# Kernel rows of two S5 blocks in one run of matmuls, an output matrix built an iteration sooner, and one buffer fewer for the gate tiles

## The chip, the cores and the metric

One core of a Trainium2 chip runs the whole kernel. A core has TensorE (PE: matmuls, with a queue of weight loads, PEld), VectorE (DVE), ScalarE (ACT), GpSimd (POOL) and SyncE (SP), each with its own queue of instructions that it takes in order; SP and POOL issue most of the DMAs here. The metric is device time in microseconds, median of several executions. A profile is one execution that the hardware profiler recorded.

## The reference

A decoder block: one input projection, a gated linear attention (GLA, four heads) and a grouped diagonal state-space layer (S5, 64 groups of 16 channels) side by side, merged by sigmoid gates, then an MLP. The change lies in S5, and in the last GLA tiles beside it:

```python
proj = xn @ w_in[l]
r = proj[..., V_END:R_END]
u = proj[..., A_END:U_END]
...
o = rmsnorm(o, gla_norm_g[l]).reshape(bsz, N_META + seq, GLA_VAL) * jax.nn.silu(r)
y_gla = o @ w_o_gla[l]
y_s = s5_ssm(pad(u), a_re[l], a_im[l], log_step[l], b_re[l], b_im[l],
             c_re[l], c_im[l], d_skip[l])[:, N_PAD:]
...
mixed = jax.nn.sigmoid(z_gla) * y_gla + jax.nn.sigmoid(z_ssm) * y_ssm
```

`s5_ssm` computes, for each group, x_t = Λ x_{t-1} + B u_t and y_t = Re(C x_t) + D u_t over 528 positions (16 meta tokens and 512 others).

## The kernel before

**Dense work.** The projections are done in slots. A slot is one tile of 128 output channels by 512 positions: 24 matmuls, since every product of two float32 numbers is made as three products of their rounded parts (high by high, high by low, low by high) over eight tiles of the contraction. A slot's weights are loaded by SP into `wraw`; ACT makes `whi`, DVE makes `wlo = wraw - whi` (line 179). Around the change the slots are of three kinds. `r0` to `r7` are GLA's gate tiles (`r_slot`, line 1307): the matmuls write a bank of `mm`; `o` (tile tag `ro`) is a tile of GLA's normalised output, read back from DRAM by SP; ACT takes the sigmoid; DVE multiplies `rs<-rs,mm` and `rs<-rs,ro`, ACT rounds the product to `ogh`, DVE makes the rest `ogl`. Then comes `z7`, a tile of merge gates, and the slots `o0` to `o7`, which multiply `ogh` and `ogl` with `w_o_gla` and use merge gates held in tiles `zt`.

**S5 blocks.** The 64 groups go in eight blocks of eight; they are counted from 0 here, so the seventh is block 6 and the eighth block 7. Positions are taken in 66 chunks of eight. `tables()` (line 1177) builds for a block, on DVE with one copy on ACT, the output matrix M2 (lines 1183 to 1191: a copy of column 0, a multiplication of 128x1024, and for each half of the groups one multiplication into `mta` and one subtraction) and the input matrix M1 (lines 1193 to 1197: two multiplications and two adds or subtractions from B and the powers `lam`). `turns()` makes the rotation table E in three steps. `kernels()` (line 1213) multiplies M2 with B's columns, BA: eight matmuls of 32 columns into one bank, copied by ACT to `krow` and `other`, joined by DVE (`COPY_PREDICATED`) and stored by POOL into `kpad` in DRAM, from which POOL loads the Toeplitz matrix M3. `scan()` multiplies M1 with the block's input U (16 small matmuls, `sm<-U,M`), rotates with E, runs the scan on DVE and gives the states X. `output()` multiplies U with M3 and X with M2; `turn_output()` transposes the result, which POOL stores.

**The loop.** Iteration b finishes block b and prepares `after`, block b+1. It runs `after.tables()` step by step between slots, then `after.turns()`, and behind the iteration's last dense slot, on PE in this order: `after.kernels()`, the U,M matmuls of `after.scan()`, and `blk.output()`. From iteration 4 (HEADS) on there are no heads of GLA left; the pool `po_` is opened there and holds `ogh`, `ogl`, `ro`, `rs` and `zt`. Blocks' tiles come from the pool `b5`, where M1, B and `krow` have one buffer and M2 has two. `wraw`, `whi` and `wlo` have three buffers each, `ro` four, and there are four banks of tag `mm` and four of `sm`.

**What sets the order.** PE's instructions keep the order of the program. On the other engines a scheduler orders the work of these iterations, from dependences and free buffers; DMAs on SP and POOL stand in the order that it gives them too. Every engine then runs its own list in order, and waits where an operand or a buffer isn't ready.

Of the kernel before, what the change touches and what calls it, by code (L numbers as in the profile page):

```python
# [17 lines left out]
P = 128  # L18
D = 1024
KT = D // P  # L20
SEQ = 512
# [4 lines left out]
HEADS = 4  # L26
# [13 lines left out]
NST = NCK - 1  # L40
GRP = 64
NST_N = 64
HG = 16
GB = 8
NBLK = GRP // GB
# [5 lines left out]
def hybrid_block(ctx: ExitStack, tc: tile.TileContext, io, out: bass.AP):  # L51
    nc = tc.nc
    V, S, G = nc.vector, nc.scalar, nc.gpsimd
# [18 lines left out]
    class InOrder:  # L72


        def __init__(self, engine):
            self.engine = engine
# [4 lines left out]
    def mk(pool, shape, dt=F32, tag=None, **kw):  # L81
        count[0] += 1
        name = f"{tag or 'x'}_{count[0]}"
        size = 1
        for n in shape[1:]:
            size *= n
        if pool not in lined or size % LINE == 0:
            return pool.tile(shape, dt, tag=tag or name, name=name, **kw)
        t = pool.tile([shape[0], -(-size // LINE) * LINE], dt, tag=tag or name, name=name, **kw)[:, :size]
        if len(shape) == 2:  # L90
            return t
        dims = " ".join("abcd"[: len(shape) - 1])
        return t.rearrange(f"p ({dims}) -> p {dims}", **dict(zip("abcd", shape[1:])))
# [425 lines left out]
    rows = mk(pxt, [P, NT], tag="xrows")  # L519
    scale_rows.append(mk(pxt, [P, T8, NCK], tag="xrowp"))  # L520
    V, S = InOrder(nc.vector), InOrder(nc.scalar)
# [219 lines left out]
    def fetch(n):  # L741
        if n < len(dense) and n not in ready:
            ready[n] = load_w(dense[n][0])[0]
# [17 lines left out]
    def slot():  # L761
        n = at[0]
        at[0] += 1
        for i in range(n, n + AHEAD + 1):
            fetch(i)
        dense[n][1](ready.pop(n))
# [63 lines left out]
    other = mk(q5, [P, GRP, HG], tag="other")  # L830
# [114 lines left out]
    b5 = pool("b5", stack=sb5, side="right")  # L945
# [7 lines left out]
    class Head:  # L953
# [199 lines left out]
        def turn_outputs(self):  # L1153
            for v in range(2):
# [5 lines left out]
                S.activation(oT, ps, AF.Copy, scale=vecs[:, V_GN + m : V_GN + m + 1])  # L1160
                nc.gpsimd.dma_start(og_dram[m], oT)

    class Block:


        def __init__(self, blk):
            self.blk = blk
            self.gs = slice(blk * GB, (blk + 1) * GB)

        def loads(self, queue=nc.sync):  # L1170

# [5 lines left out]
        def tables(self):  # L1177

            M1 = self.M1 = mk(b5, [P, GB, 2, NST_N], tag="M1", bufs=1)
            self.M2 = mk(b5, [P, GB, 9, HG], tag="M2", bufs=2)  # L1180
            B, (lr, li) = self.B, (self.lam[:, i].unsqueeze(2).to_broadcast([P, GB, 2, NST_N]) for i in range(2))
            sh = [P, GB, T8, HG]
            S.copy(self.M2[:, :, 0], CA[:, self.gs])
            lrb, lib = (L[:, 1:, self.gs].rearrange("p l g -> p g l").unsqueeze(3).to_broadcast(sh) for L in (Lr, Li))
            ca, cb = (C[:, self.gs].unsqueeze(2).to_broadcast(sh) for C in (CA, CB))
            V.tensor_mul(self.M2[:, :, 1:], ca, lrb)
            for g0 in (0, 4):
                gg = slice(g0, g0 + 4)
                ta = mk(b5, [P, 4, T8, HG], tag="mta")
                V.tensor_mul(ta, cb[:, gg], lib[:, gg])  # L1190
                V.tensor_sub(self.M2[:, gg, 1:], self.M2[:, gg, 1:], ta)
                yield
            V.tensor_mul(M1, B, lr)
            yield
            V.tensor_mul(B, B, li)
            V.tensor_sub(M1[:, :, 0], M1[:, :, 0], B[:, :, 1])
            self.made = V.tensor_add(M1[:, :, 1], M1[:, :, 1], B[:, :, 0])
            yield

        def turns(self):  # L1200

# [11 lines left out]
        def kernels(self, tag="sm"):  # L1213

            ps = bank(tag)
            for j in range(GB // 2):
                for e in range(2):
                    g = 2 * j + e
                    PE.matmul(ps[32 * j : 32 * j + 32, e * P : (e + 1) * P], BA[:, self.blk * GB + 2 * j : self.blk * GB + 2 * j + 2, :].rearrange("p g h -> p (g h)"), self.M2[:, g, 0:8, :].rearrange("p l h -> p (l h)"), start=True, stop=True)
            krow = mk(b5, [P, P], tag="krow", bufs=1)  # L1220
            other = mk(b5, [P, GB, NST], tag="v", bufs=1).rearrange("p g c -> p (g c)")[:, :P]
            S.copy(krow, ps[:, :P])
            S.copy(other, ps[:, P : 2 * P])
            V.copy_predicated(krow, odd, other)
            V.scalar_tensor_tensor(krow[:, :HG], i16, vecs[:, V_D + self.blk : V_D + self.blk + 1], krow[:, :HG], op0=ALU.mult, op1=ALU.add)
            nc.gpsimd.dma_start(kpad[self.gs].rearrange("g h l -> (g h) l")[:, 112:], krow)
# [80 lines left out]
    def r_slot(m):  # L1307
        def go(w):
            ps = bank("mm")
            feat_tile(w, xh, xl, NM, NT, ps)  # L1310
            o = mk(po_, [P, SEQ], tag="ro", bufs=4)
            nc.sync.dma_start(o, og_dram[m])
            sg_ = mk(po_, [P, SEQ], tag="rs", bufs=2)
            S.activation(sg_, ps, AF.Sigmoid)
            V.tensor_mul(sg_, sg_, ps)
            V.tensor_mul(sg_, sg_, o)
            split_hi(ogh[:, m], sg_)
            V.tensor_sub(ogl[:, m], sg_, f32(ogh)[:, m])

        dense.append((cols("w_in", C_R + m * P), go))  # L1320
# [16 lines left out]
    heads, blocks = [], [Block(b) for b in range(NBLK)]  # L1337
# [63 lines left out]
    V, S = nc.vector, nc.scalar  # L1401
    for b, blk in enumerate(blocks):
        if not b:
            continue
        this = heads[b] if b < HEADS else None
        last = heads[b - 1] if 0 < b <= HEADS else None
        after = blocks[b + 1] if b + 1 < NBLK else None
        if b == 1:
            with tc.issue_after(heads[0].held.ins):
                list(blk.turns())  # L1410
        following = after.tables() if after else iter(())
        slot()
        early = b < HEADS + 1 or not after
        if b > 1:
            if early:
                blocks[b - 1].turn_output()
            if b == 2:
                heads[0].turn_outputs()
            next(steps)
        if this:  # L1420
            this.decay_load()
            with tc.issue_after(this.taken.ins), tc.issue_after(heads[0].held.ins), tc.issue_after(last.keyed.ins):
                list(this.decays())
        if b > 1:
            if after:
                after.loads()
            next(following, None)
        slot()
        if b == 1:
            blk.kernels("mm")  # L1430
            steps = blk.scan()
            next(steps)
            blocks[0].output("mm")
            blk.kernel_loads()
        list(steps)
        if not early:
            blocks[b - 1].turn_output()
        if b == 1:
            after.loads()
        if last:  # L1440
            last.outputs()
            if not this:
                last.normalised()
        if this:
            with tc.issue_after(this.taken.ins):
                this.query_decay()
        next(following, None)
        if b < NBLK - 1:
            slot()
        if this:  # L1450
            with tc.issue_after(this.kept.ins):
                last.normalised()
            this.turn_values()
        next(following, None)
        if after:
            list(after.turns())
        slot()
        if this:
            this.turn_keys()
        if b == 1:  # L1460
            blocks[0].turn_output(tag="mm")
        if last and b > 1:
            last.turn_outputs()
        if b == HEADS:
            sgb.close()
            sg.close()
            so = ExitStack()
            po_ = pool("po", stack=so, padded=True)
            ogh = mk(po_, [P, KT, SEQ], F32R, tag="ogh")
            ogl = mk(po_, [P, KT, SEQ], F32R, tag="ogl")  # L1470
        for _ in range(2):
            next(following, None)
        if after:
            slot()
        if this:
            this.scores("mm")
        if after:
            after.kernels()
            steps = after.scan()
            next(steps)  # L1480
        blk.output("mm" if this else "sm")
        if after:
            after.kernel_loads()
        if this:
            this.states()
            this.split()
    slot()
    blocks[-1].turn_output(last=True)
    while at[0] < len(dense):
# [107 lines left out]
    for c4, c in enumerate(range(0, D, 256)):  # L1597
        ss_ = []
        parts = out_weights(c4, dict(raw_))
        for i, w in enumerate(load_w(wg[:, D + c : D + c + 256])):  # L1600
# [5 lines left out]
            zt = mk(pgl, [P, SEQ], tag="zi", bufs=2)  # L1606
# [161 lines left out]
    V, S = InOrder(nc.vector), InOrder(nc.scalar)  # L1768
# [110 lines left out]
    V, S = nc.vector, nc.scalar  # L1879
# [62 lines left out]
    po_ = pool("pout", side="right", padded=True)  # L1942
# [178 lines left out]
```

## Time and profile before

| | |
|---|---|
| median of 3 runs | 856.58 us (856.49 to 856.67) |
| the profiled execution | 856.36 us |
| its span, first to last instruction | 854.6 us |
| mean granted clock of TensorE | 0.998 |
| ACT busy | 466.1 us (55%) |
| POOL busy | 150.9 us (18%) |
| DMA, mean over the span | 225 GB/s |

The median is of unprofiled runs, the span of the one that was recorded; 856.36 − 854.6 = 1.76 us of it lie around the span. Blocks 6 and 7 are prepared between about 290 and 352 us of the span. In the rows, names of tiles are without their numbers, and both M1 and M2 (and M3) are called M: `M<-CA,Lr` and `M<-M,mta` are M2, `M<-B,lam` and `M<-M,B` are M1, `sm<-M,BA` are kernel rows (M2), `sm<-U,M` the scan's input (M1), `sm<-M,U` and `sm<-M,X` the output (M3, M2). A row of the timeline has start and duration in us, engine, line, operation, what is written from what is read, and in brackets how long the engine was idle before and who ended that.

### The profile page before, as it was taken

The page shows a single profiled execution, that of the slowest core. Times are in us where ns is not written, and L with a number is a line of the kernel's source. Part 1 is how long each engine was busy: PE and PEld are TensorE (multiplying, and loading weights), DVE is VectorE, ACT ScalarE, POOL GpSimd, SP SyncE. Part 2 cuts the span into 40 slices and gives each one's busy share as a digit, 9 for nine tenths or more (in the row PEclk, how much of TensorE's full clock was granted, in tenths as well). Part 3 has the DMA queues.
Part 4 walks back from the last instruction along what each step waited for, and adds up shares of the span by engine and source line. Part 5 has one row for each costly group of instructions (what it writes and reads, how often), then busy time and mean ns, then how long its engine had stood idle before and what let it go on. Part 6 is the DMA issues. An engine that isn't in the chain of part 4 may idle for free.

```text
span 854.6 us, 13817 instructions
## 1 busy us (share of the span) xinstructions
PE 845.5 (99%) x4974; PEld 725.7 (85%) x4974; DVE 688.9 (81%) x1282; ACT 466.1 (55%) x832; POOL 150.9 (18%) x265
## 2 busy tenths in 40 slices
PE   9999999999999999999999999999999999999996
PEld 8998889898988888888888889888888888888885
DVE  6999889998989599846888687667666777688886
ACT  7677465766856546334555466333222246885763
POOL 1123120240303123240222421011111100000001
PEclk9999999999999999999999999999999999999999
DMA  9887765566565765686898996498989967766564
GB/s 316 194 279 225 226 148 150 141 162 178 138 165 153 242 187 144 223 267 204 242 281 265 280 281 217 134 331 289 346 280 333 363 218 243 267 192 197 172 200 145
DMA packets 172492, 192.67 MB, mean 225 GB/s; under 512 B 18648, under 2 KB 127720, under 8 KB 172424
## 3 DMA queue, kind: packets, MB, share of 16 engines
q1 hardware_dynamic: 145040, 109.66, 44.3%
q0 software_dynamic: 25408, 77.93, 27.4%
q10 hardware_dynamic: 1976, 4.20, 1.6%
q8 instruction: 39, 0.64, 0.3%
q14 instruction: 29, 0.24, 0.1%
HBM read 149.52 MB, written 42.24 MB: 224 GB/s over the span
## 4 chain that ended last, share of the span: by engine, by line
PE 96%; DMA 2%; DVE 1%; ACT 0%; issue 0%; SPq 0%; DVEq 0%; ACTq 0%
PE mm L61 72%; PE sm L61 22%; PE sm L66 2%; DMA wraw<-in_w_in_dram 2%; DMA xT<-in_x_cols_dram 1%; DVE c L2041 0%; DVE c L2016 0%; DVE wlo L79 0%; ACT whi L79 0%; DVE rl L79 0%; DVE xT L79 0%; ACT rh L79 0%; DVEq L2117 0%; SPq L478 0%; DVE ff_r L150 0%
## 5 line engine op out<-in xcount | busy, mean ns | idle before, releaser
L164 ACT ACTIVATE whi<-wraw 128x1024 fp32r<-128x1024 f32 x81 | 85.8, 1059 | 180.4 <-PE mm L61 171.2
L61 PE MATMUL mm<-xh,whi 128*128 128x512 f32 (+2 forms) x464 | 157.5, 339 | 0.0
L61 PE MATMUL mm<-xh,wlo 128*128 128x512 f32 (+2 forms) x464 | 155.2, 335 | 0.0
L61 PE MATMUL mm<-xl,whi 128*128 128x512 f32 (+2 forms) x464 | 155.1, 334 | 0.0
L179 DVE TENSOR_TENSOR wlo<-wraw,whi 128x1024 fp32r<-128x1024 f32 x81 | 98.9, 1223 | 69.1 <-ACT whi L164 69.0
L61 PE MATMUL mm<-hh,whi 128*128 128x512 f32 (+2 forms) x272 | 100.7, 370 | 0.0
L61 PE MATMUL mm<-hh,wlo 128*128 128x512 f32 (+2 forms) x272 | 100.6, 370 | 0.0
L61 PE MATMUL mm<-hl,whi 128*128 128x512 f32 (+2 forms) x272 | 100.6, 370 | 0.0
L61 PEld LDWEIGHTS mm<-xh,wlo 128*128 128x128 f32 x464 | 87.4, 188 | 9.0
L61 PEld LDWEIGHTS mm<-xh,whi 128*128 128x128 f32 x464 | 87.3, 188 | 8.8 <-issue 0.3
L61 PEld LDWEIGHTS mm<-xl,whi 128*128 128x128 f32 x464 | 87.3, 188 | 8.5
L1959 DVE TENSOR_TENSOR wlo<-wraw,whi 128x1024 fp32r<-128x1024 f32 x56 | 68.4, 1223 | 22.4 <-ACT whi L1955 22.2
L61 PE MATMUL sm<-wlo,fh 128*128 128x512 f32 x192 | 74.8, 390 | 0.0
L61 PE MATMUL sm<-whi,fl 128*128 128x512 f32 x192 | 74.7, 389 | 0.0
L61 PE MATMUL sm<-whi,fh 128*128 128x512 f32 x192 | 74.7, 389 | 0.0
L1955 ACT ACTIVATE whi<-wraw 128x1024 fp32r<-128x1024 f32 x56 | 58.7, 1050 | 17.1 <-PE mm L61 11.7
L61 PEld LDWEIGHTS mm<-hh,whi 128*128 128x128 f32 x272 | 51.1, 188 | 8.8
L61 PEld LDWEIGHTS mm<-hl,whi 128*128 128x128 f32 x272 | 51.1, 188 | 8.7
L61 PEld LDWEIGHTS mm<-hh,wlo 128*128 128x128 f32 x272 | 51.1, 188 | 8.7
L164 ACT ACTIVATE fh<-f 128x512 fp32r<-128x512 f32 x48 | 30.2, 629 | 36.1 <-PE sm L61 22.3
L61 PE MATMUL mm<-gh,whi 128*128 128x512 f32 x128 | 49.8, 389 | 0.0
L61 PE MATMUL mm<-gl,whi 128*128 128x512 f32 x128 | 49.8, 389 | 0.0
(537 smaller groups left out, 1880.8 us busy)
## 6 DMA issues: line engine op xcount, KB each, us to landing
wraw<-in_w_ff_dram SPq DMA_DIRECT2D x56, 512.0 KB
wraw<-in_w_in_dram SPq DMA_DIRECT2D x46, 512.0 KB
w2raw<-in_w_ff_dram POOLq DMA_DIRECT2D x16, 1024.0 KB, 8.8
t2d<-w2t POOLq DMA_DIRECT2D x16, 1024.0 KB, 6.0
wraw<-t2d SPq DMA_DIRECT2D x32, 512.0 KB
wraw<-in_w_glu_dram SPq DMA_DIRECT2D x16, 512.0 KB
M<-kpad POOLq DMA_DIRECT2D x64, 64.0 KB, 2.6
wraw<-in_w_o_gla_dram SPq DMA_DIRECT2D x8, 512.0 KB
```

The lines of the kernel that those rows point to most:

```text
L61: ins = nc.tensor.matmul(*args, **kw)
L66: ins = nc.tensor.transpose(*args, **kw)
L164: return S.activation(dst, src, AF.Copy, scale=scale)
L179: V.tensor_sub(lo, raw, f32(hi))
L1955: halved = S.activation(bh, raw, AF.Copy)
L1959: V.tensor_sub(bl, raw, f32(bh))
```

## The change

Four edits belong together.

- The part of `tables()` that builds M2 becomes a generator of its own, `outward(pl)`, which can take its tile from another pool. For block 7 it is run in whole at the end of iteration 4, from `po_`, with one buffer; `tables()` of block 7 then builds M1 alone, in iteration 6 as before.
- In iteration 5 block 7's kernel rows are made right behind block 6's, into a bank of tag `mm`. In iteration 6 `kernels()` is not called.
- The rows of block 7 go into a `zt` tile of `po_` (columns 0 to 127 for the rows, 128 to 255 for the other half) instead of `krow` and `v`.
- `ro` has three buffers instead of four.

```diff
+    JOINED = NBLK - 1
...
         def tables(self):
 
             M1 = self.M1 = mk(b5, [P, GB, 2, NST_N], tag="M1", bufs=1)
-            self.M2 = mk(b5, [P, GB, 9, HG], tag="M2", bufs=2)
             B, (lr, li) = self.B, (self.lam[:, i].unsqueeze(2).to_broadcast([P, GB, 2, NST_N]) for i in range(2))
+            if not self.M2:
+                yield from self.outward(b5)
+            V.tensor_mul(M1, B, lr)
+            yield
+            V.tensor_mul(B, B, li)
+            V.tensor_sub(M1[:, :, 0], M1[:, :, 0], B[:, :, 1])
+            self.made = V.tensor_add(M1[:, :, 1], M1[:, :, 1], B[:, :, 0])
+            yield
+
+        def outward(self, pl):
+
             sh = [P, GB, T8, HG]
+            self.M2 = mk(pl, [P, GB, 9, HG], tag="M2", bufs=2 if pl is b5 else 1)
             S.copy(self.M2[:, :, 0], CA[:, self.gs])
...
                 V.tensor_sub(self.M2[:, gg, 1:], self.M2[:, gg, 1:], ta)
                 yield
-            V.tensor_mul(M1, B, lr)
-            yield
-            V.tensor_mul(B, B, li)
-            V.tensor_sub(M1[:, :, 0], M1[:, :, 0], B[:, :, 1])
-            self.made = V.tensor_add(M1[:, :, 1], M1[:, :, 1], B[:, :, 0])
-            yield
...
-            krow = mk(b5, [P, P], tag="krow", bufs=1)
-            other = mk(b5, [P, GB, NST], tag="v", bufs=1).rearrange("p g c -> p (g c)")[:, :P]
+            if self.blk == JOINED:
+                rows = mk(po_, [P, SEQ], tag="zt", bufs=6)
+                krow, other = rows[:, :P], rows[:, P : 2 * P]
+            else:
+                krow = mk(b5, [P, P], tag="krow", bufs=1)
+                other = mk(b5, [P, GB, NST], tag="v", bufs=1).rearrange("p g c -> p (g c)")[:, :P]
...
-            o = mk(po_, [P, SEQ], tag="ro", bufs=4)
+            o = mk(po_, [P, SEQ], tag="ro", bufs=3)
...
         if after:
-            after.kernels()
+            if after.blk != JOINED:
+                after.kernels()
+            if b == JOINED - 2:
+                blocks[JOINED].kernels("mm")
             steps = after.scan()
...
+        if b == HEADS:
+            list(blocks[JOINED].outward(po_))
```

What this does to the order of instructions is seen in the built programs. Names carry numbers here; `mm_739` is a bank, M1, M2 and M3 are told apart.

On PE, behind the last dense slot of iteration 5, stands before (the second line is block 6's kernel rows, eight matmuls):

```order
L61 MATMUL mm_730_4223<-xh_7_100,wlo_709_4109 128x512
L61 MATMUL sm_733_4256<-M2_695_4040,BA_14_110 32x128 x8
L61 MATMUL sm_738_4274<-U_714_4148,M1_694_4039 64x65 x8
L61 MATMUL sm_739_4286<-U_714_4148,M1_694_4039 64x65 x8
L61 MATMUL sm_740_4298<-M3_685_3983,U_651_3792 64x128 x2
```

and at the same place in the changed program, where `M2_686` is block 7's output matrix:

```order
L61 MATMUL mm_733_4232<-xh_7_100,wlo_712_4118 128x512
L61 MATMUL sm_736_4265<-M2_698_4049,BA_14_110 32x128 x8
L61 MATMUL mm_739_4281<-M2_686_3992,BA_14_110 32x128 x8
L61 MATMUL sm_743_4298<-U_717_4157,M1_697_4048 64x65 x8
L61 MATMUL sm_744_4310<-U_717_4157,M1_697_4048 64x65 x8
L61 MATMUL sm_745_4322<-M3_685_3983,U_651_3792 64x128 x2
```

The third line has moved here from behind the last dense slot of iteration 6, where dense work is now followed by the scan's matmuls at once. The number of matmuls is the same.

On DVE, around the last operations of block 6's M1 (its two adds, `M1<-M1,B`), before:

```order
L1196 TENSOR_TENSOR M1_694_4039<-M1_694_4039,B_692_4034 128x8x64
L1318 TENSOR_TENSOR ogl_668_3875<-rs_712_4138,ogh_667_3874 128x512
L241 TENSOR_TENSOR E_713_4146<-mta_717_4163,epb_718_4164 128x8x16
L242 TENSOR_TENSOR E_713_4146<-mta_717_4163,epb_718_4164 128x8x16
L1197 TENSOR_TENSOR M1_694_4039<-M1_694_4039,B_692_4034 128x8x64
L239 TENSOR_TENSOR mta_719_4169<-E_713_4146 128x512
L240 TENSOR_TENSOR epb_720_4170<-E_713_4146 128x512
L1315 TENSOR_TENSOR rs_726_4208<-rs_726_4208,mm_724_4181 128x512
L241 TENSOR_TENSOR E_713_4146<-mta_719_4169,epb_720_4170 128x8x32
L242 TENSOR_TENSOR E_713_4146<-mta_719_4169,epb_720_4170 128x8x32
L1316 TENSOR_TENSOR rs_726_4208<-rs_726_4208,ro_725_4206 128x512
L179 TENSOR_TENSOR wlo_729_4221<-wraw_727_4217,whi_728_4219 128x1024
```

and in the changed program:

```order
L241 TENSOR_TENSOR E_716_4155<-mta_720_4172,epb_721_4173 128x8x16
L242 TENSOR_TENSOR E_716_4155<-mta_720_4172,epb_721_4173 128x8x16
L1328 TENSOR_TENSOR rs_729_4217<-rs_729_4217,ro_728_4215 128x512
L239 TENSOR_TENSOR mta_722_4178<-E_716_4155 128x512
L240 TENSOR_TENSOR epb_723_4179<-E_716_4155 128x512
L1330 TENSOR_TENSOR ogl_668_3875<-rs_729_4217,ogh_667_3874 128x512
L241 TENSOR_TENSOR E_716_4155<-mta_722_4178,epb_723_4179 128x8x32
L242 TENSOR_TENSOR E_716_4155<-mta_722_4178,epb_723_4179 128x8x32
L1189 TENSOR_TENSOR M1_697_4048<-M1_697_4048,B_695_4043 128x8x64
L1190 TENSOR_TENSOR M1_697_4048<-M1_697_4048,B_695_4043 128x8x64
L179 TENSOR_TENSOR wlo_732_4230<-wraw_730_4226,whi_731_4228 128x1024
L1327 TENSOR_TENSOR rs_735_4259<-rs_735_4259,mm_733_4232 128x512
```

The adds stood among the second rotation step, `rs` and `ogl`; now they stand behind the last rotation step, that `rs` and an `ogl` which came after the wlo. Between one and the same wlo further up (`wlo_688` before, `wlo_691` now, shown next) and the second add there are 54 rows where from that wlo through the `rs<-rs,ro` shown there were 50.

On DVE, some fifty rows earlier, at the start of that stage, before:

```order
L179 TENSOR_TENSOR wlo_660_3823<-wraw_658_3819,whi_659_3821 128x1024
L179 TENSOR_TENSOR wlo_671_3883<-wraw_669_3879,whi_670_3881 128x1024
L179 TENSOR_TENSOR wlo_688_3996<-wraw_686_3992,whi_687_3994 128x1024
L1315 TENSOR_TENSOR rs_674_3912<-rs_674_3912,mm_672_3885 128x512
L1224 COPY_PREDICATED krow_676_3927<-odd_18_114,v_677_3928 128x128
```

and in the changed program:

```order
L179 TENSOR_TENSOR wlo_660_3823<-wraw_658_3819,whi_659_3821 128x1024
L179 TENSOR_TENSOR wlo_671_3883<-wraw_669_3879,whi_670_3881 128x1024
L1200 TENSOR_TENSOR M2_686_3992<-CA_12_108,Lr_10_106 128x8x128
L1205 TENSOR_TENSOR M2_686_3992<-M2_686_3992,mta_687_3995 128x4x128
L179 TENSOR_TENSOR wlo_691_4005<-wraw_689_4001,whi_690_4003 128x1024
L1327 TENSOR_TENSOR rs_674_3912<-rs_674_3912,mm_672_3885 128x512
```

Two operations of block 7's M2 (`M2_686`) now stand ahead of that wlo.

More of the change, by code (lines that the diff above doesn't have):

```diff
@@ L1168, in __init__ @@
             self.gs = slice(blk * GB, (blk + 1) * GB)
+            self.M2 = None
         def loads(self, queue=nc.sync):
```

## The prediction

> **What bounds the kernel now.** I read the page first: the busy table and the chain of work that ended last.
>
> ```profile
> PE 845.5 (99%) x4974; PEld 725.7 (85%) x4974; DVE 688.9 (81%) x1282; ACT 466.1 (55%) x832; POOL 150.9 (18%) x265
> ...
> PE 96%; DMA 2%; DVE 1%; ACT 0%; issue 0%; SPq 0%; DVEq 0%; ACTq 0%
> ```
>
> TensorE (PE) is busy for 845.5 us of the 854.6 us span, and 96% of the chain that ended last is PE. Next I asked for the waits of PE, whole run, and then for busy time by window around the two places that the diff moves: 289.7 to 321.2 us is the stage that ends with block 6's kernel rows, 321.2 to 351.5 us the one that ends with block 7's.
>
> ```profile
> PE sm L61 <- DVE xss L517: 1.3, 1, 1.3
> PE sm L61 <- DVE xrs L79: 0.4, 1, 0.4
> ```
>
> ```profile
> core 0: us, PE busy (x) PEld busy (x) DVE busy (x) ACT busy (x) POOL busy (x), PEclk, DMA share, GB/s
> 289.70:321.20 31.50, 31.50 (x216) 26.00 (x214) 30.86 (x52) 15.77 (x29) 7.18 (x13) 1.00 0.68 207
> 321.20:351.50 30.30, 30.30 (x182) 25.04 (x178) 29.45 (x49) 14.27 (x27) 7.75 (x14) 1.00 0.62 180
> ```
>
> PE waits for other engines twice, both near the start (xss and xrs belong to the first norm). In the two stages it never stops. So the time changes in two ways only: PE's own instruction stream gets shorter or longer, or somebody is now late for PE. The candidate is VectorE (DVE): busy 30.86 of 31.50 us in the first stage, so nearly every operation put into it pushes out all that stands behind.
>
> **PE's own stream.** The change leaves all instructions and moves eight small matmuls. PE's timeline at three places, start and duration:
>
> ```profile
> 319.81 0.39 PE L61 MATMUL mm<-xh,wlo 128*128 128x512 f32 x1
> 320.13 0.67 PE L61 MATMUL sm<-M,BA 128*32 128x128 f32 x16
> 320.73 0.69 PE L61 MATMUL sm<-U,M 128*64 128x65 f32 x16
> ...
> 351.16 0.39 PE L61 MATMUL mm<-ogh,wlo 128*128 128x512 f32 x1
> 351.48 0.66 PE L61 MATMUL sm<-M,BA 128*32 128x128 f32 x16
> 352.07 0.34 PE L61 MATMUL sm<-U,M 128*64 128x65 f32 x4
> ...
> 371.67 0.39 PE L61 MATMUL mm<-ogh,wlo 128*128 128x512 f32 x1
> 371.99 0.44 PE L61 MATMUL sm<-M,U 128*64 128x128 f32 x4
> ```
>
> The record count is twice that of the program (each of the eight is two records). In the second place the run goes: from the last dense matmul to the scan's matmuls are 352.07 − 351.16 = 0.91 us before. Afterwards dense work is followed by a 64-column group at once; the third place shows that pair, 371.99 − 371.67 = 0.32. Saving **0.59 us**; bounds 0 (the whole gap stays) and 0.91.
>
> In the first place the run of 16 records becomes 32. The sixteen matmuls last 0.67 from first start to last end; a single one lasts 0.28 (mean of the form, below), so fifteen steps take 0.39, 0.026 each, and sixteen more steps cost **+0.42 us**. If the two banks' runs met as badly as M,BA meets U,M (first start to first start 0.60, of which 16 steps are 0.42, so 0.18 more), it would be +0.60; if they overlapped as much as possible, 0.39. By itself PE's stream comes out at 0.42 − 0.59 = **−0.17 us** (to +0.01 with the worse seam).
>
> ```profile
> L61 PE MATMUL sm<-M,BA 128*32 128x128 f32 x112 | 4.6, 279 | 0.0
> ```
>
> [...]
>
> **The new wait.** The scan's matmuls U,M read M1, block 6's input matrix, whose last two operations are the adds `M<-M,B`. DVE, in the first stage:
>
> ```profile
> 289.72 1.22 DVE L179 TENSOR_TENSOR wlo<-wraw,whi 128x1024 fp32r<-128x1024 f32 x1 [5.13 <-ACT whi L164]
> ...
> 296.24 0.69 DVE L1285 TENSOR_TENSOR qt<-q,sm 128x512 f32<-128x512 f32 x1 [0.48 <-ACT q L1283]
> ...
> 298.67 0.68 DVE L1190 TENSOR_TENSOR mta<-CB,Li 128x512 f32<-128x512 f32 x1
> 299.27 1.24 DVE L1258 TENSOR_TENSOR_SCAN v<-d,v 128x520 f32<-128x520 f32 x1
> ...
> 314.66 0.69 DVE L1196 TENSOR_TENSOR M<-M,B 128x512 f32<-128x512 f32 x1
> ...
> 316.27 0.69 DVE L1197 TENSOR_TENSOR M<-M,B 128x512 f32<-128x512 f32 x1
> ...
> 319.34 0.70 DVE L1316 TENSOR_TENSOR rs<-rs,ro 128x512 f32<-128x512 f32 x1
> 319.94 1.23 DVE L179 TENSOR_TENSOR wlo<-wraw,whi 128x1024 fp32r<-128x1024 f32 x1
> ```
>
> Before, the last add ends at 316.27 + 0.69 = 316.96, and PE takes U,M at 320.73: 3.8 us to spare. In the changed order both adds stand behind the last rotations, the next `rs<-rs,ro` and an `ogl`. From the wlo of 289.72 to the second add, both included, stand 54 rows: all 50 that stood from that wlo through 319.34, and four more (two `mta<-CB,Li`, one `M<-M,mta`, one `ogl<-rs,ogh`). Each such 128x512 operation takes 299.27 − 298.67 = 0.60 of DVE. Before, the 50 rows were through at 319.94. Four more make 2.40; the hole of 0.48 ahead of qt is filled, as two of the four now stand ready there. DVE is through at 319.94 + 2.40 − 0.48 = 321.86, and as an operation ends some 0.10 after the next may start (0.70 long, step 0.60), M1 is whole at **321.96** (322.44 if the hole stays).
>
> PE would want U,M at 320.73 + 0.42 = 321.15. It waits about 0.8 us, and with a few hundredths of signalling I take **+0.85** (bounds 0.4 and 1.35: one operation less in between, or the hole kept). Behind the waiting matmul stand U,M, the block output and the next dense run, that is all of PE, so the wait is paid in full and carried to the end, since PE waits nowhere later.
>
> Sum: +0.42 + 0.85 − 0.59 = **+0.68 us**. While there is a wait, the seam does not count: U,M starts when M1 is whole.
>
> **Edits that I cost at nothing.** The first two operations of block 7's output matrix on DVE stand in the idle 5.13 us ahead of 289.72. They take 1.13 and 0.60:
>
> ```profile
> 329.06 1.22 DVE L1186 TENSOR_TENSOR M<-CA,Lr 128x1024 f32<-128x1024 f32 x1
> 330.19 1.24 DVE L1258 TENSOR_TENSOR_SCAN v<-d,v 128x520 f32<-128x520 f32 x1
> ```
>
> If that cover were gone, M1 would be 1.73 later, and so would PE. The copies on ACT (column 0 of M2, two copies of rows) lie on an engine that is busy 15.77 of 31.50 us. POOL stores block 7's rows earlier, at 7.18 busy of 31.50. With three buffers for ro, a gate tile's load may be issued when the `rs<-rs,ro` three slots back is through; those stand some 5.6 us apart (313.72 and 319.34), so 16.8 us remain for an issue and a landing, and the longest median landing in the page's table of DMA issues is 11.4:
>
> ```profile
> 313.72 0.69 DVE L1316 TENSOR_TENSOR rs<-rs,ro 128x512 f32<-128x512 f32 x1
> ...
> woraw<-in_w_out_dram POOLq DMA_DIRECT2D x8, 512.0 KB, 5.0
> ...
> wraw<-tdo POOLq DMA_DIRECT2D x4, 512.0 KB, 11.4
> ```
>
> SP handles the loads in order, so a late ro would also hold the wraw behind it; it has the same 16.8 us.
>
> **The second place and block 7's B.** B has one buffer, so block 7's load waits for block 6's last add, and it moves with it:
>
> ```profile
> 316.99 0.60 SPq L895 DMA_DIRECT2D B<-bard  x1
> ...
> DMA to landing us min/median/max: 7.7/7.7/7.7
> ...
> 341.37 0.70 DVE L1318 TENSOR_TENSOR ogl<-rs,ogh 128x512 fp32r<-128x512 f32 x1
> ...
> 345.50 0.39 PE L61 MATMUL mm<-ogl,whi 128*128 128x512 f32 x1
> ```
>
> It was issued at 316.99, right behind the add; now at about 322.0. The one B load whose landing is shown took 7.7, so B is there at 329.7 (327.0 to 333.4 by the 5.0 and 11.4 of other 512 KB loads). In the new order `M<-B,lam` stands 14 rows behind the last add. Those are two wlo (319.94, the next operation of before starts at 321.08: 1.14), six of 0.60, the two halves of v (0.67 together) and the row operations of two blocks (0.20 + 0.15 each):
>
> ```profile
> 321.08 0.69 DVE L1318 TENSOR_TENSOR ogl<-rs,ogh 128x512 fp32r<-128x512 f32 x1
> ...
> 324.02 0.31 DVE L1224 COPY_PREDICATED krow<-odd,v 128x128 f32<-128x128 int32 x1
> 324.22 0.70 DVE L1316 TENSOR_TENSOR rs<-rs,ro 128x512 f32<-128x512 f32 x1
> 324.82 0.24 DVE L1225 SCALAR_TENSOR_TENSOR krow<-i,vecs,krow 128x16 f32<-128x16 f32 x1
> 324.97 0.77 DVE L1252 TENSOR_TENSOR v<-sm,E 128x260 f32<-128x260 f32 x2
> 325.64 0.69 DVE L1282 SCALAR_TENSOR_TENSOR q<-q,sm 128x512 f32<-128x512 f32 x1
> ```
>
> Together 7.25 us, so DVE gets there at about 329.1 and waits **0.6 us** (0 to 4.3). Does PE notice? Behind it on DVE is the last `ogl`, which PE reads first at 345.50, later by 0.42 + 0.85: 346.8. Counted from 319.94 as before, the work up to that ogl loses 4.1 us (five M2 operations, one ogl) and gains 2.7 (B's multiplication, two adds, two row operations); from 321.86 that ends at about 342.5 without the wait. So 4.2 us are free and I put down **0**.
>
> The profiled execution took 856.36, 0.22 under the median of 856.58. 856.36 + 0.68 = 857.04, on the median **857.3**.
>
> **The rivals.**
> - **No new wait**: DVE gains enough (rows that waited for ACT or PE before, or an earlier start) to finish M1 by 321.15. It needs 0.8 us, more than the hole of 0.48 already spent. Then −0.17: 856.4 (856.6 with the worse seam). Against it: the four operations are in the order and 30.86 of 31.50 is busy.
> - **Slower, by block 7's B**: the load lands late enough to hold DVE past its 4.2 us, that is after 329.1 + 4.2 = 333.3, 11.3 us past its issue. Then PE waits at the first ogl, us for us: at 13 us, 1.7 more, in all +2.4, 859.0. For it: landings of 11.4 exist at this size. Against: the only B load seen took 7.7, and the DMA share is 0.62 there.
> - **The second place saves nothing**: the scan's matmuls start no sooner behind dense work (the 0.91 was the change of shape, not the run). Then +0.42 + 0.85 = +1.27: 857.9. Against: 0.32 at 371.67.
>
> **How the numbers follow.** Forecast of a short wait (856.8 to 857.9): 0.76. No new wait: 0.12. Block 7's B: 0.06. No saving: 0.06. The range 856.2 to 858.4 takes in the first, the second and the fourth. 0.2% of the time, about what a measurement can tell from no change, is 1.7 us: faster is below 854.9, slower above 858.3. The forecast and the no-wait case lie within; slower is B's case and some 0.03 of a longer wait: 0.09. Faster needs a gain that no row shows: 0.03.
>
> **What would show it.** Right: a wait of PE on DVE's add of M1 (line 1190 of the new kernel) of 0.5 to 1.3 us near 321, thirty-two records of M,BA in a row, U,M about 0.3 behind dense work at the second place, B's load near 322 and a wait at `M<-B,lam` that nobody on PE answers. Wrong: no wait of PE there; a wait at the first ogl of the slots behind; a wlo that PE waits for; or a wait of 2.5 us, which would mean that the idle 5.13 us didn't cover M2's first operations.

## The result and the profile after

| | before | after |
|---|---|---|
| median of 7 runs | 856.58 us (856.26 to 856.67) | 859.30 us (857.22 to 860.86) |
| the profiled execution | 856.36 us | 860.06 us |
| its span | 854.6 us | 858.3 us |
| mean granted clock of TensorE | 0.998 | 0.995 |

The ratio of the runs is 1.0030, 95% interval 1.0020 to 1.0039: slower by about 2.6 us (the medians differ by 2.72). The runs of before lie within 0.41 us of each other; those of the changed kernel spread over 3.64. In the two later sessions the kernel before spread over 1.72 (29 runs) and 0.65 (13 runs).

The waits of PE for its whole run, after (engine and line waited for: us in total, times, longest):

```profile
PE sm L61 <- issue: 1.6, 1, 1.6
PE sm L61 <- DVE xss L517: 1.3, 1, 1.3
PE sm L61 <- DVE xrs L79: 0.3, 1, 0.3
PE sm L61 <- DVE M L1190: 0.3, 1, 0.3
PE sm L61 <- DVE wlo L79: 0.2, 1, 0.2
```

Three were not in the list of before. The last of them lies in the first 30 us, and the kernel with M1 early (first experiment), which loses nothing, has it too. The other two, "issue" and L1190, matter; PE's timeline shows both at one place, behind the joined kernel rows:

```profile
320.21 0.66 PE L61 MATMUL sm<-M,BA 128*32 128x128 f32 x16
320.67 0.66 PE L61 MATMUL mm<-M,BA 128*32 128x128 f32 x16
322.90 0.30 PE L61 MATMUL sm<-U,M 128*64 128x65 f32 x2 [1.57 <-issue]
323.45 1.09 PE L61 MATMUL sm<-U,M 128*64 128x65 f32 x29 [0.26 <-DVE M L1190]
...
327.85 0.55 PE L61 MATMUL mm<-xh,whi 128*128 128x512 f32 x1
```

The first half of M1 comes at 322.80 and lets two matmuls go (the view writes "issue", but they are the ones that read it, and in the kernel with the early matrix only it names the add, L1189); the second comes at 323.40 and lets the rest go. The next dense matmul starts at 327.85, 4.40 after that. The granted clock explains a part of these 4.40; busy time by window, the clock is the number behind the last bracket:

```profile
core 0: us, PE busy (x) PEld busy (x) DVE busy (x) ACT busy (x) POOL busy (x), PEclk, DMA share, GB/s
...
323.00:324.00 1.00, 0.74 (x20) 0.61 (x22) 1.00 (x2) 0.00 (x0) 0.00 (x0) 1.00 0.15 51
324.00:325.00 1.00, 1.00 (x29) 1.00 (x25) 1.00 (x2) 0.00 (x0) 0.00 (x0) 0.79 0.11 41
325.00:326.00 1.00, 1.00 (x12) 1.00 (x10) 1.00 (x4) 0.03 (x1) 0.00 (x0) 0.50 0.51 160
326.00:327.00 1.00, 1.00 (x14) 1.00 (x12) 0.99 (x4) 0.60 (x1) 0.57 (x1) 0.50 0.51 131
327.00:328.00 1.00, 1.00 (x10) 0.67 (x6) 0.81 (x3) 0.04 (x1) 0.23 (x1) 0.51 0.63 146
328.00:329.00 1.00, 1.00 (x5) 0.82 (x6) 0.41 (x1) 0.96 (x3) 0.31 (x1) 1.00 1.12 228
```

PE pays a second time: about a microsecond after the wait its clock is halved, for 3.4 us (the four windows lack 0.21 + 0.50 + 0.50 + 0.49 = 1.70 us of full clock). The page's line for the clock still shows nines there; only the fine windows tell.

DVE, which PE waits for, through the same stage:

```profile
284.58 1.22 DVE L1200 TENSOR_TENSOR M<-CA,Lr 128x1024 f32<-128x1024 f32 x1
285.83 0.69 DVE L1205 TENSOR_TENSOR M<-M,mta 128x512 f32<-128x512 f32 x1
289.80 1.23 DVE L179 TENSOR_TENSOR wlo<-wraw,whi 128x1024 fp32r<-128x1024 f32 x1 [3.27 <-ACT whi L164]
...
291.54 0.30 DVE L1236 COPY_PREDICATED krow<-odd,v 128x128 f32<-128x128 int32 x1
293.00 0.69 DVE L1328 TENSOR_TENSOR rs<-rs,ro 128x512 f32<-128x512 f32 x1 [1.17 <-DMA ro<-og]
...
295.63 0.69 DVE L1204 TENSOR_TENSOR mta<-CB,Li 128x512 f32<-128x512 f32 x1
296.66 0.69 DVE L1297 TENSOR_TENSOR qt<-q,sm 128x512 f32<-128x512 f32 x1 [0.35 <-ACT q L1295]
...
298.48 1.22 DVE L1200 TENSOR_TENSOR M<-CA,Lr 128x1024 f32<-128x1024 f32 x1
...
322.72 0.68 DVE L1190 TENSOR_TENSOR M<-M,B 128x512 f32<-128x512 f32 x1
```

and the rows of before at the same place:

```profile
291.46 0.29 DVE L1224 COPY_PREDICATED krow<-odd,v 128x128 f32<-128x128 int32 x1
291.89 0.69 DVE L1316 TENSOR_TENSOR rs<-rs,ro 128x512 f32<-128x512 f32 x1
...
294.54 1.22 DVE L1186 TENSOR_TENSOR M<-CA,Lr 128x1024 f32<-128x1024 f32 x1
```

Block 7's first two operations do lie in the idle stretch ahead of the wlo, which still has 3.27 us of its 5.13 left. But DVE then waits 1.17 for the first `ro` tile, where the profile of before shows no wait (it stood 0.14 there, from 291.75 to 291.89, and the view puts that down to nobody), and the hole ahead of `qt` stays.

The second place, dense work straight into the scan's matmuls:

```profile
355.50 0.39 PE L61 MATMUL mm<-ogh,wlo 128*128 128x512 f32 x1
355.82 0.57 PE L61 MATMUL sm<-U,M 128*64 128x65 f32 x12
```

0.32 instead of 0.91, as forecast. The difference between the two profiled executions, 3.70 us, is then made of: 0.08 from a slightly later start of the stage (320.21 against 320.13), 0.44 for the longer run of kernel rows (how it is measured: first experiment), 2.20 of wait (323.45, where PE without a wait would have been at 320.21 + 0.60 + 0.44 = 321.25; of these 2.20 PE stood idle for 1.57 + 0.26 = 1.83), 1.57 for the slow clock (4.40 where 2.83 is enough; below), and −0.59: together 3.70.

### The profile page after: what moved, and what is told of

It reads as the page before. It is cut to its first block, busy times and chain, and to the rows that moved or that the text cites. A ratio compares the mean times of both kernels' runs of the same rounds, so it can differ in the third digit from the quotient of the medians.

```text
span 858.3 us, 13818 instructions
## 1 busy us (share of the span) xinstructions
PE 847.3 (99%) x4974; PEld 727.3 (85%) x4974; DVE 689.8 (80%) x1282; ACT 465.8 (54%) x832; POOL 151.4 (18%) x265
## 4 chain that ended last, share of the span: by engine, by line
PE 94%; DMA 2%; DVE 2%; issue 0%; ACT 0%; ACTq 0%; DVEq 0%
PE mm L61 71%; PE sm L61 22%; PE sm L66 2%; DMA wraw<-in_w_in_dram 2%; DMA xT<-in_x_cols_dram 1%; DVE c L2058 0%; DVE ogl L1330 0%; DVE c L2033 0%; DVE rs L1328 0%; DVE wlo L79 0%; DVE epb L240 0%; DVE B L1188 0%; DVE wlo L179 0%; ACT whi L79 0%; ACT whi L164 0%
```

## The experiments

After the profile the theory was: the early output matrix pushes M1 of block 6 back on DVE, PE idles for it, and that idle time also halves PE's clock. The rivals: the joined rows, the third `ro` buffer or block 7's late B cost by themselves; and the slow stretch comes from the small matmuls or from memory traffic, not from idling.

### M1 finished ahead of the rotations

```diff
+        if b == JOINED - 2:
+            list(following)
         if after:
             list(after.turns())
```

> The changed kernel, with block 6's input matrix M1 finished ahead of block 6's rotations (its adds stand 16 rows earlier on DVE). Theory: all of the loss is PE's wait for M1 and what that wait sets off; without it PE's own stream remains, -0.2 to 0 us against before: 856.4 to 856.7, no wait of PE near 321, granted clock 1.00 throughout. Rival: the joined rows, the single late load of block 7's B or the third ro buffer cost by themselves; then 857.5 or more stays, with PE waiting elsewhere.

Measured: 856.15 us (11 runs, 855.84 to 856.65), before in the same session 856.39; ratio 0.9996 (0.9987 to 1.0004). PE has no wait between 280 and 400 us, and its clock is 1.00 from 280 to 333 us. Its timeline:

```profile
319.88 0.66 PE L61 MATMUL sm<-M,BA 128*32 128x128 f32 x16
320.34 0.66 PE L61 MATMUL mm<-M,BA 128*32 128x128 f32 x16
320.92 1.15 PE L61 MATMUL sm<-U,M 128*64 128x65 f32 x32
323.75 0.50 PE L61 MATMUL mm<-xh,whi 128*128 128x512 f32 x1
```

From the first kernel row to U,M are 1.04 us, 0.60 before: the longer run costs 0.44, and the seam between the banks is as long as the steps within them (by single records of the changed kernel's profile, where the two banks also start 0.46 apart, they come in fours, 0.11 apart, across the seam too: 320.45 and 320.56 in the first bank, 320.67 and 320.78 in the second). From U,M to dense work are 2.83, as before (320.73 to 323.56). With everything else of the change in, the time is that of before, or a little under, which this many runs can't tell. So the joined rows and the third `ro` buffer cost nothing that shows by themselves. Block 7's B is not late here: its load is issued right behind M1's last add (add over at 316.96 and load at 316.99 before, 323.40 and 323.43 in the changed kernel), and that add stands 16 rows earlier on DVE; that its lateness cost nothing in the changed kernel is seen in that kernel's own profile, where DVE takes B without a wait (below). DVE waited 1.6 us for the first `ro` here too, and it cost nothing, as PE had no wait for M1.

### PE kept busy during the wait

```diff
                 blocks[JOINED].kernels("mm")
+                fill = bank("mm")
+                for _ in range(8):
+                    PE.matmul(fill, xh[:, 0, :P], xh[:, 0, NM:NT], start=True, stop=True)
```

> The changed kernel with eight extra 128x512 matmuls (into a bank that nobody reads) behind the joined kernel rows, 1.8 us of PE work inside the wait of 2.2 us. Theory (idle PE halves the granted clock): the wait stays, M1 comes at the same time, but the clock stays at 1.00 and the 1.6 us of slow matmuls are not paid: 858.0 to 858.6, the runs close together. Rival (the slow stretch belongs to the small matmuls or to the memory traffic there): the stretch at 0.50 stays, 859 to 861 as in the changed kernel, spread over 3 us.

Measured: 858.49 us (11 runs, 857.84 to 859.77), under the changed kernel's 859.30 although PE does more. Its ratio to before is 1.0022 (1.0014 to 1.0031), and that interval overlaps the changed kernel's, so the times alone don't tell the two apart. The clock stays at 1.00 from 318 to 330 us in the profile, PE shows no wait there, and the profiled run took 858.12. Dense work starts 6.24 after the first kernel row (326.00 − 319.76); less the 2.83 from U,M to dense work, PE was let go 3.41 after that row, 3.24 in the changed kernel (323.45 − 320.21), so no earlier. The upper end of the spread is above what was expected (859.77 against 858.6); those runs were not profiled.

### Four buffers for ro again

```diff
-            o = mk(po_, [P, SEQ], tag="ro", bufs=3)
+            o = mk(po_, [P, SEQ], tag="ro", bufs=4)
...
-                zt = mk(po_, [P, SEQ], tag="zt", bufs=6)
+                zt = mk(po_, [P, SEQ], tag="zt", bufs=5)
```

The smaller `zt` (in three places, of which one is shown) makes room.

> The changed kernel with four buffers for ro again and five for zt instead of six. Theory: the wait of 1.2 us for the first ro is the chance of one landing, not of the buffer count; time as of the changed kernel, 858 to 861, a wait of PE of 1 to 2.3 us. Rival: the third buffer's loss delays ro; then the wait of DVE on ro goes, M1 comes 1.2 us earlier, PE waits about 1.0 and the time falls to 857.3 or lower.

Measured: 858.15 us (11 runs, 857.81 to 861.02); the wait of DVE for the first `ro` is still there, 0.9. The profiled run took 858.15, and is the changed kernel without the slow clock:

```profile
322.57 0.30 PE L61 MATMUL sm<-U,M 128*64 128x65 f32 x2 [1.29 <-issue]
323.12 1.09 PE L61 MATMUL sm<-U,M 128*64 128x65 f32 x29 [0.25 <-DVE M L1190]
...
325.95 0.50 PE L61 MATMUL mm<-xh,whi 128*128 128x512 f32 x1
```

The wait cost 1.92 us here (323.12, less 320.16 + 0.60 + 0.44), 0.28 less than in the changed kernel's profile (PE stood idle for 1.29 + 0.25 = 1.54 of it), the clock stayed at 1.00, and U,M to dense work took 2.83 instead of 4.40. Two of its eleven runs took 859.49 and 861.02. So the buffer count is not the cause of that wait. The kernel's ratio to before is 1.0022 (1.0013 to 1.0030), that of the changed kernel 1.0030 (1.0020 to 1.0039): the intervals overlap, and no difference is claimed.

### Only the three-buffer edit, in the kernel before

```diff
-            o = mk(po_, [P, SEQ], tag="ro", bufs=4)
+            o = mk(po_, [P, SEQ], tag="ro", bufs=3)
```

> The kernel before with three buffers for ro and nothing else; DVE's order is that of before. Theory: the buffer count costs nothing and does not delay the first ro (it lands near 291.8, DVE doesn't wait for it): 856.2 to 856.7. Rival (the count delays the loads): the first ro lands about 1.1 us later and DVE waits for it, though the 3.8 us to spare hide it from the time.

Measured: 856.59 us (10 runs, 855.84 to 857.76), ratio 1.0004 (0.9995 to 1.0013). The waits of DVE from 285 to 323.5 us:

```profile
DVE wlo L179 <- ACT whi L164: 8.0, 2, 5.1
DVE rs L1316 <- DMA ro<-og: 1.0, 1, 1.0
DVE qt L1285 <- ACT q L1283: 0.5, 1, 0.5
```

No loss that can be measured. The wait for the first `ro` is in it, which by itself would speak for the rival. But three kernels further down have four buffers and DVE's order of before up to that point; they waited 0, 1.0 and 1.1. So DVE can wait a microsecond for the first `ro` with four buffers and the old order too. The profiles come from two sessions on two chips, though. On the one, the old order waits 0 (one profile) and kernels with the change's order 0.9 to 1.6 (three); on the other, the old order waits 1.0 to 1.1 (three) and the early matrix 0.7 (one). The wait needs no change; whether the change lengthens it is not shown.

### Only the early matrix, the rows not joined

```diff
-            if after.blk != JOINED:
-                after.kernels()
-            if b == JOINED - 2:
-                blocks[JOINED].kernels("mm")
+            after.kernels()
```

> Block 7's output matrix early and three buffers for ro as in the change, but block 7's kernel rows at their old place in iteration 6. Theory (the early matrix alone moves DVE's order, and so makes the wait): M1 of block 6 is whole at the same time as in the changed kernel, PE stands ready 0.45 us sooner, so the wait is 2.3 to 2.7 us, the 0.6 at the second place isn't saved: 858.6 to 861.5. Rival (the joined run makes the loss): 856.5 to 857.

Measured: 859.54 us (4 runs, 859.29 to 859.72), before 856.27 in the same session; ratio 1.0039 (1.0024 to 1.0054).

```profile
319.66 0.66 PE L61 MATMUL sm<-M,BA 128*32 128x128 f32 x16
321.87 0.30 PE L61 MATMUL sm<-U,M 128*64 128x65 f32 x2 [1.54 <-DVE M L1189]
322.42 1.49 PE L61 MATMUL sm<-U,M 128*64 128x65 f32 x29 [0.26 <-DVE M L1190]
...
326.89 0.50 PE L61 MATMUL mm<-xh,whi 128*128 128x512 f32 x1
```

The whole loss is there without any joined row: PE is ready at 319.66 + 0.60 = 320.26 and gets M1 at 322.42, 2.16 later, and the way to dense work takes 4.47 under a clock of 0.50. DVE waited 0.7 for `ro` here, which is why the wait is a little under the 2.3 to 2.7 expected.

### The same loss made in the kernel before, and the clock alone

The second half of block 6's M1 is copied onto itself on DVE, two or three times, so that M1 is whole later; its values stay, and nothing of the change is in. With three copies a second version gives PE 13 extra matmuls into a bank that nobody reads, ahead of U,M.

```diff
             self.made = V.tensor_add(M1[:, :, 1], M1[:, :, 1], B[:, :, 0])
+            for _ in range(3 if self.blk == 6 else 0):
+                V.tensor_copy(M1[:, :, 1], M1[:, :, 1])
...
             after.kernels()
+            if after.blk == 6:
+                fill = bank("mm")
+                for _ in range(13):
+                    PE.matmul(fill, xh[:, 0, :P], xh[:, 0, NM:NT], start=True, stop=True)
```

> The kernel before, with M1 of block 6 copied onto itself twice on DVE, which makes it whole at about 322.3 to 322.9 instead of 317.0; PE then waits 1.6 to 2.1 us for it, and nothing else of the change is in. Theory (a wait of this size also halves the clock, in some runs): 858.2 to 858.7 where it doesn't, up to 1.6 more where it does, and rows at 0.50 in a slow run. Rival (only the wait counts): 858.2 to 858.7 in every run.

Two copies: 860.12 us, 6 runs: 857.97, 858.73, 859.31 and, after a gap, 860.93, 861.33, 861.82. The profiled one is the fastest: 1.38 of idle, the clock at 1.00, DVE without a wait for `ro`. The upper three were not profiled, so that their clock was halved is not shown; they lie above the expected 860.3 by up to 1.5.

> The kernel before with three copies of M1 onto itself; M1 is whole at about 323.8 and PE waits 3.0 us. Theory (idle PE halves the granted clock for a few us): every run is gated, 856.4 + 3.0 + 1.6 = 861.0 or more, a stretch of 0.50 right behind the wait. Rival (only the wait counts): 859.4.

Three copies: 862.34 us (4 runs, 861.67 to 863.40); before in the same session 856.27. PE went on with U,M at 325.18, where M1 had been expected whole at 323.8, as the stage began 0.30 later than in the profile of before and DVE waited 1.0 for the first `ro`.

> The same three copies, and 13 extra 128x512 matmuls (3.2 us) into a bank that nobody reads, ahead of the matmuls that wait. Theory (idle PE halves the clock): the clock stays at 1.00, 859.4 to 859.9 in every run, 1.5 us or more under the same kernel without the extra matmuls. Rival (not idleness): the stretch at 0.50 and its 1.6 us stay.

With PE kept busy: 859.98 us (4 runs, 859.91 to 860.27), 2.36 us less for a kernel with 13 matmuls more; the four runs of the one all lie above the four of the other. They are a little over the 859.4 to 859.9 expected; the `ro` wait was 1.1 here. PE's timeline of three copies, and then of the version with the extra matmuls:

```profile
320.43 0.67 PE L61 MATMUL sm<-M,BA 128*32 128x128 f32 x16
...
325.18 1.89 PE L61 MATMUL sm<-U,M 128*64 128x65 f32 x29 [3.82 <-DVE M L1199]
...
329.49 0.50 PE L61 MATMUL mm<-xh,whi 128*128 128x512 f32 x1
```

```profile
319.95 0.66 PE L61 MATMUL sm<-M,BA 128*32 128x128 f32 x16
...
324.75 1.09 PE L61 MATMUL sm<-U,M 128*64 128x65 f32 x29 [0.68 <-DVE M L1199]
...
327.58 0.50 PE L61 MATMUL mm<-xh,whi 128*128 128x512 f32 x1
```

Both reach U,M equally late, 4.75 and 4.80 after the first kernel row. From there to dense work the one takes 4.31, with U,M at 1.89 for what lasts 1.09, and the other 2.83. The same matmuls, in the same place, on the same data: what differs is whether PE idled before. So 1.48 us are the price of the clock, and the rival falls: the small matmuls are the same, and the DMA traffic in the microsecond in which U,M goes on was no lower in the kernel that kept its clock (316 GB/s, 324 to 325 us, against 270, 325 to 326); with two copies the clock was 1.00 under 302 GB/s (323 to 324), in the changed kernel 0.79 under 41 (324 to 325). The other 0.5 of the difference between the two profiled runs is an earlier start of the stage, 319.95 against 320.43.

## Why the prediction was wrong

The sum gave +0.68 us; the two profiled executions differ by 3.70. Of the 3.02 in between, 1.35 is the wait that was too small, 1.57 the clock that was left out, 0.08 a later start of the stage and 0.02 the longer run of kernel rows.

**The place and the kind of the loss were right.** A new wait of PE for M1 at U,M, from DVE's order, with the second place's saving intact: all in the trace, and "early matrix only" and "M1 ahead of the rotations" show that this order alone decides.

**PE's own stream: right.** +0.42 and −0.59 were forecast, 0.44 and −0.59 measured (0.91 − 0.32). That the seam between the two banks counts as one more step was an estimate, as no row of before shows such a seam; measured in the changed kernel's profile, it is 0.11 us, as between the fours inside a bank (the step of 0.026 that the prediction used is their average). The kernel with M1 early shows the net: 0.24 under before where −0.17 was worked out, though its interval includes no change.

**The wait: the failed step.** It was worked out as 0.85 with bounds 0.4 and 1.35; the profile has 2.20, outside the bounds. The four extra operations were there. Wrong was the sentence that DVE would be through at "319.94 + 2.40 − 0.48 = 321.86": it took from the one profile of before that DVE waits in that stage for nothing but ACT. M1 was whole at 323.40, 1.44 after the 321.96 of the prediction. Three things make that: the first `ro` landed 1.17 after DVE asked for it; the hole ahead of `qt` stayed at 0.35 (the prediction had the hole kept as an end of its range); the stage began 0.08 later. Together 1.60. Of these, 0.16 come off: 0.14 that DVE had stood ahead of the same `rs<-rs,ro` before, which the prediction's sum held, and 0.02 by which the last add was shorter. The operations themselves took what was predicted: without waits, 54 rows make 32.00 us, and 50 rows and four of 0.60 make 29.60 + 2.40. The few hundredths allowed for signalling were 0.05 (323.40 to 323.45).

The hole was misread too. The prediction had it filled by two operations that now stand ready there. The rows show one, `mta<-CB,Li` at 295.63 (0.60), while block 6's longer `M<-CA,Lr` (1.14), which stood ahead of `qt` before (294.54), moved behind it (298.48). And what ends the hole came later: ACT began that `q` at 296.00, at 295.58 before.

The prediction's own sign for a longer wait, an idle stretch that doesn't cover M2's first operations, is not what happened: 3.27 us of that stretch were left.

The wait for `ro` needs no change. It stands in the profiles of seven of the eight experiments, 0.7 to 1.6 us, three of them with DVE's order of before (three buffers, three copies, three copies with extra matmuls); with two copies and in the profile of before the view shows none. Whether the change adds to it stays open, as said. Before, 3.8 us of slack on M1 lay behind it, and nobody paid. The change spent the slack and so passes the lateness on.

**What the prediction left out altogether: the clock.** It let a wait cost its own length. In the three profiles with 1.80 us of idle PE or more, the way to dense work took 1.48 to 1.64 us longer than 2.83:

| profile | PE idle ahead of U,M's bulk | clock behind it | U,M to dense work |
|---|---|---|---|
| with extra matmuls (13) | 0.68 | 1.00 | 2.83 |
| two copies | 1.38 | 1.00 | 2.83 |
| four `ro` buffers | 1.54 | 1.00 | 2.83 |
| early matrix only | 1.80 | 0.50 | 4.47 |
| the change | 1.83 | 0.50 | 4.40 |
| three copies | 3.82 | 0.50 | 4.31 |

(Idle is the sum of what the brackets of the rows show; where two short matmuls run in between, two brackets are added. It is less than what the wait costs, 2.20 in the change.) With one profile of each, no threshold is claimed. This gives the spread of the changed kernel's runs a reading: where `ro` lands in time, PE loses about a microsecond, and the sum of the prediction holds (the fastest run took 857.22, forecast 857.3); where it lands late, PE loses 2.2 and pays 1.6 more, 860 to 861. That the runs sort themselves so is argued from the profiled ones; the others were not profiled. The mean clock on record for each run points that way: 0.995 or 0.996 in the three runs above 860, 0.997 or 0.998 in the other four. It is no proof: the profiled run with the early matrix only has its slow stretch at a mean of 0.997.

**Block 7's B: right that PE wouldn't notice.** It was issued at 323.43, and DVE took `M<-B,lam` at 332.03 without a wait, as PE's slow stretch had held up what stands ahead. The wait of 0.6 for it didn't come.

**Three buffers for `ro`, the copies, POOL's order: nothing, as forecast**, for the buffers by the kernel with three buffers alone (1.0004, 0.9995 to 1.0013), for all of them together by the kernel with M1 early (0.9996, 0.9987 to 1.0004). Why the first `ro` lands where it does is open; loading it a slot earlier, which would tell, was not tried.

## What to carry to other kernels

Slack that no profile counts can be what hides a transfer's jitter (here the first `ro`, for which DVE waited 0 to 1.6 us): before an edit spends it, ask what else stood behind it, and look at that spot in more than one profile. Price a new wait of TensorE with what follows it: here the three profiles with 1.80 us of idle or more were charged again by half the clock for 3.4 us, the three with 1.54 or less were not. If operations are moved forward on a busy in-order engine, finish first what the next engine needs: the same change with M1 ahead of the rotations lost nothing.

## What the runs showed of the hardware

The slow stretch has the same length in all three profiles that have it: the windows lack 1.70 us of full clock in the change, 1.71 with the early matrix only, 1.71 with three copies, that is 3.4 us at one half. For the last of these, where the slow clock begins ahead of the first matmul that it slows:

```profile
324.00:325.00 1.00, 0.00 (x0) 0.00 (x0) 1.00 (x2) 0.00 (x0) 0.00 (x0) 0.97 1.04 251
325.00:326.00 1.00, 0.82 (x15) 0.82 (x17) 1.00 (x4) 0.00 (x0) 0.00 (x0) 0.50 0.90 270
326.00:327.00 1.00, 1.00 (x23) 1.00 (x23) 1.00 (x3) 0.44 (x1) 0.04 (x1) 0.50 0.70 204
327.00:328.00 1.00, 1.00 (x13) 1.00 (x11) 0.80 (x3) 0.94 (x4) 0.53 (x1) 0.50 0.91 267
328.00:329.00 1.00, 1.00 (x20) 1.00 (x18) 1.00 (x3) 0.73 (x2) 0.00 (x0) 0.82 0.32 108
```

In the three, PE idled 1.83, 1.80 and 3.82 us ahead of U,M. What sets the length of the stretch no run shows.
